# Thirty-two or sixty-four bytes more behind the weight tiles and the normed input's halves

## The chip, the cores and the metric

The kernel runs on one core of a Trainium2 chip. The metric is the device time of one execution in microseconds. Of the other cores none has work.

## The reference, cut to what matters

One layer of a hybrid decoder block on 256 tokens of width 2048, all in float32. Four large blocks of products follow each other, each behind an RMS norm:

```python
h = h + 0.5 * swiglu(rms_norm(h, ffn1_norm), ffn1_w_gu, ffn1_w_down)   # 2048 -> 2 x 5632 -> 2048
h = h + hybrid_mixer(rms_norm(h, mix_norm), w_in, ..., w_out)          # 2048 -> 7184 -> 2048
h = h + 0.5 * swiglu(rms_norm(h, ffn2_norm), ffn2_w_gu, ffn2_w_down)
gate = jax.nn.sigmoid(rms_norm(h, ple_norm) @ ple_w_gate)              # 2048 -> 2048
h = h + gate * (p @ ple_w_proj)                                        # 256 -> 2048
return rms_norm(h, final_norm)
```

The mixer holds a gated delta rule on eight heads and a stick-breaking attention on eight more; its own small products lie between the large ones.

## The kernel before, in words

Every large product is y = x @ w with 256 tokens in x. The tokens are the output's rows, in two tiles of 128; the columns of w go in blocks of 512, and the inner dimension in k-tiles of 128. TensorE has a stationary operand, which a weight load (LDWEIGHTS) brings in, and a moving one, which the matmul streams. Here **the stationary operand is x** (128 x 128, one k-tile of one tile of tokens) **and the moving operand is w** (128 x 512). So each matmul needs a weight load of its own, which runs beside the matmul ahead of it.

Both operands are split into two float32r halves, hi + lo, and three of the four products are taken: x_hi w_hi (line 73), x_hi w_lo (line 74) and x_lo w_hi (line 75). For the last block of columns of the last product lines 85 to 87 do the same for one tile of tokens after the other.

`weight_pair` (line 49) brings two k-tiles of a weight block, 512 KB, from DRAM into `raw` (four buffers, SyncE's queue), ScalarE rounds it to `whi` (line 59), and VectorE subtracts to get `wlo` (line 60). `whi` and `wlo` have three buffers each, so ScalarE and VectorE can be two pairs ahead of TensorE. `accumulate` (line 63) then issues 12 matmuls for the pair: two k-tiles, two tiles of tokens, three products.

The stationary halves have other names by stage. `nTh` and `nTl` are the normed and transposed input of a stage, four tiles each of four k-tiles, made by `new_nT` (line 109); they are used by the outputs `g` and `u` (gate and up columns of an FFN), `pj` (the mixer's input projection), `gt` (the last gate) and by the small `abT` (line 465, where `nTh` and `nTl` move and a padded tile `wpad` is stationary). `hTh` and `hTl` are the FFN's inner activations, used by `d`. `dnT` and `sbT` are the mixer's head outputs, used by `wo`. `ph` and `pl` are the embedding's input, used by `e`.

Between the pairs of a product a list of generators (`lanes`) puts in the pieces of other work: VectorE's transposes of the FFN's activations (line 127), the norms, and the mixer's heads. The order of instructions on each engine is the order in which the code emits them; tile pools give out the buffers, and a tile that is wanted again waits for the last reader of its buffer.

Tiles stand in each partition one behind the other in the order in which a pool first sees their tags, each at a multiple of 32 bytes. The sizes of nearly all large tiles are multiples of 512 bytes, so that all buffers of a tag, and all tags of a pool, have the same start modulo 512. In the built program the starts in bytes of a partition, modulo 512, are:

| tiles | operand of the large products | start modulo 512 |
|---|---|---|
| `raw`, `whi`, `wlo` | moving | 480 in all buffers |
| `nTh`, `nTl` | stationary of g, u, pj, gt | 480 in all tiles |
| `hTh`, `hTl` | stationary of d | 224 in all tiles |
| `dnT`, `sbT` | stationary of wo | 384 in all tiles |
| `ph`, `pl` | stationary of e | 224 |
| `wpad` | stationary of abT | 448 |
| `whi`, `wlo` of the last column block | moving, lines 85 to 87 | 224 in all buffers |

Inside a tile an operand starts at a multiple of 512 bytes from the tile's start, so a row of the table holds for every matmul of its stage.

Of the kernel before, what the change touches and what calls it, by code (L numbers as in the profile page):

```python
# [16 lines left out]
P = 128  # L17
T = 256
# [11 lines left out]
def block_kernel(ctx, tc, a, out):  # L30
# [17 lines left out]
    # ---------------------------------------------------------------- weights  # L48
    def weight_pair(src, pool=wp, bufs=3, parts=1):
        """Two k-tiles of a weight block, split into float32r halves hi + lo, in one or two parts."""  # L50
        raw = wp.tile([P, 2, NB], F32, tag="raw", name="raw", bufs=4)
        hi = pool.tile([P, 2, NB], F32R, tag="whi", name="whi", bufs=bufs)
        lo = pool.tile([P, 2, NB], F32R, tag="wlo", name="wlo", bufs=bufs)
        for i in range(parts):
            j = slice(2 * i // parts, 2 * (i + 1) // parts)
            nc.sync.dma_start(out=raw[:, j, :], in_=src[:, j, :])
        for i in range(parts):
            j = slice(2 * i // parts, 2 * (i + 1) // parts)
            nc.scalar.copy(hi[:, j, :], raw[:, j, :])  # L59
            nc.vector.tensor_tensor(out=lo[:, j, :], in0=raw[:, j, :], in1=hi[:, j, :], op=ALU.subtract)  # L60
        return hi, lo

    def accumulate(outs, xs, wsrc, nk, parts=1):
        """outs[t] += x[:, t].T @ w over nk k-tiles; xs(k) gives (hi, lo) [P, T]."""
        for g in range(nk // 2):
            whi, wlo = weight_pair(wsrc[g], parts=parts if g == 0 else 1)
            for j in range(2):
                k = 2 * g + j
                xh, xl = xs(k)
                for t in range(2):  # L70
                    c = slice(t * P, (t + 1) * P)
                    st, sp = k == 0, k == nk - 1
                    nc.tensor.matmul(outs[t], xh[:, c], whi[:, j, :], start=st, stop=False)  # L73
                    nc.tensor.matmul(outs[t], xh[:, c], wlo[:, j, :], start=False, stop=False)  # L74
                    nc.tensor.matmul(outs[t], xl[:, c], whi[:, j, :], start=False, stop=sp)  # L75
            lanes.step()

    def products(ps_t, t, xs, ws, n):
        """ps_t = x[:, t].T @ w[:, n] for one tile of tokens, with the pairs of weight tiles ws."""
        for g, (whi, wlo) in enumerate(ws):  # L80
            for j in range(2):
                k = 2 * g + j
                xh, xl = xs(k)
                c = slice(t * P, (t + 1) * P)
                nc.tensor.matmul(ps_t, xh[:, c], whi[:, j, n], start=k == 0, stop=False)
                nc.tensor.matmul(ps_t, xh[:, c], wlo[:, j, n], start=False, stop=False)
                nc.tensor.matmul(ps_t, xl[:, c], whi[:, j, n], start=False, stop=k == 2 * len(ws) - 1)

    # keeps the tensor engine's clock up until the first weights are there
# [6 lines left out]
    # ---------------------------------------------------------------- inputs  # L96
# [11 lines left out]
    # ---------------------------------------------------------------- norms  # L108
    def new_nT():
        hi = [act.tile([P, 4, T], F32R, tag="nTh", name="nTh", bufs=4) for _ in range(4)]  # L110
        lo = [act.tile([P, 4, T], F32R, tag="nTl", name="nTl", bufs=4) for _ in range(4)]
        return hi, lo
# [9 lines left out]
    def transpose_blocks(dst, src, q):  # L122
        """Tokens 32*q.. of both tiles: src [tokens, tile, 512] -> dst [column, k-tile, token], by 32 x 32."""
        for c in range(4):
            sv = src[32 * q:32 * q + 32].rearrange("p t (j c x) -> p t j c x", j=4, c=4)[:, :, :, c, :]
            dv = dst[32 * c:32 * c + 32].rearrange("p j (t q x) -> p t j q x", t=2, q=4)[:, :, :, q, :]
            nc.vector.transpose(dv, sv)  # L127

    def norm_block_behind(nT, which, j, tmp):
        """norm_block on the vector engine, emitted behind the next products."""  # L130
# [11 lines left out]
    def norm_block(nT, which, j, tmp):  # L142
        """Transposes columns j*512.. of h, times the norm's gain, into nT."""
# [29 lines left out]
    def rstd(stat, t=None):  # L173
        """1/sqrt(mean of h^2 + eps) by token, [P, 2] for both tiles or [P, 1] for tile t."""
# [8 lines left out]
    # ---------------------------------------------------------------- FFN  # L183
# [52 lines left out]
    # first norm: the transposed input comes from DRAM, its parts one after the other  # L236
# [43 lines left out]
    # ---------------------------------------------------------------- mixer  # L280
# [6 lines left out]
    # the embeddings' input, split ahead of its use  # L287
# [10 lines left out]
    # ---------------------------------------------------------------- per-layer embedding, last norm  # L298
    with tc.tile_pool(name="fin", bufs=1) as fp:
# [6 lines left out]
        def gated(e, gt, c, t, col):  # L306
            """Adds sigmoid(gt) * e to the columns c of h; their sum of squares into column col of stat."""
# [19 lines left out]
        # last columns: one tile of tokens after the other  # L327
# [18 lines left out]
class Lanes:  # L346
    """Work that is emitted piece by piece between the pairs of weight tiles of the large products."""
# [23 lines left out]
def mixer(tc, nc, a, act, mm_ps, mx_ps, accumulate, picker, new_nT, norm_block, sumsq, block, lanes,  # L371
# [5 lines left out]
    with tc.tile_pool(name="mix", bufs=1) as mp, \  # L377
            tc.tile_pool(name="dram", bufs=1, space=bass.MemoryType.DRAM) as dp:
        # ------------------------------------------------------------ constants
        one = mp.tile([P, 1], F32, tag="one", name="one")  # L380
        nc.gpsimd.memset(one, 1.0)
        # tri[j, i] = 1 where j <= i in the same half of 64
# [13 lines left out]
        # inverses of the triangular systems and (in part) their transposes, by tile and head: what is  # L396
        # below (above) the diagonal stays 0
# [5 lines left out]
        def natural(blk):  # L403
            """Columns blk*512.. of the input projection, [tokens, columns], two tiles."""
            o = [mm_ps("pj") for _ in range(2)]
            accumulate(o, xs, a["w_in"][blk], KD)
            return o
# [9 lines left out]
        def transpose_pair(nat, pr):  # L417
            """[tokens, 4 heads] -> PSUM [d, heads 2*pr and 2*pr+1, tokens]."""
# [13 lines left out]
        def bc(x):  # L432
            """[P, 4] -> [P, 4, 128], the same along the last axis."""
            return x.rearrange("p (c o) -> p c o", o=1).broadcast_to([P, 4, P])
# [13 lines left out]
        # ------------------------------------------------------------ decay and beta  # L448
# [5 lines left out]
        def decay_and_beta():  # L454
            wab = mp.tile([P, KD, 16], F32, tag="sol", name="wabr")
            nc.scalar.dma_start(out=wab, in_=a["w_ab"])
            # stationary columns: hi parts in 0..15, lo parts in 32..47
# [31 lines left out]
            # softplus(x) = max(x, 0) + ln(1 + exp(-|x|))  # L489
# [11 lines left out]
            # running sums of g inside halves of 64, and the sums of both halves  # L501
# [9 lines left out]
            # sB: running sum as seen from the second half; eG: exp of the sum from the tile's start;  # L511
            # eT: exp of the sum from here to the tile's end
# [9 lines left out]
        # ------------------------------------------------------------ gated delta rule: q, k, v of 4 heads  # L522
# [69 lines left out]
        # ------------------------------------------------------------ gated delta rule: the chain  # L592
# [4 lines left out]
        def chain(hg):  # L597
            hs = slice(hg * 4, hg * 4 + 4)
            kq, v, o = knq[hg], vn_[hg], o_nat[hg]
            # dec[j, t, head, i] = exp(sum of g over (j, i]), 0 where i < j  # L600
# [13 lines left out]
            # keys of the first tile, decayed to its end  # L614
            nc.vector.tensor_tensor(out=v3(kdec[hg]), in0=v3(kdec[hg]), in1=bc(eT[:, 0, hs]), op=ALU.mult)
            # AT[j, i] = (k_j . q_i) dec;  N[j, i] = -beta_j (k_j . k_i) dec
# [16 lines left out]
            # the diagonal blocks of 32, one per 4 partitions: [block (t c b), column group], rows x columns  # L633
# [12 lines left out]
            # forward substitution, 8 columns of an inverse in a partition  # L646
# [22 lines left out]
            # blocks of 32 -> blocks of 64  # L669
# [17 lines left out]
            # blocks of 64 -> 128  # L687
# [17 lines left out]
            # first tile: u = beta * (Z^T v); o = A u; state = k_dec^T u  # L705
# [13 lines left out]
            # second tile  # L719
# [18 lines left out]
            # o = rq d^-0.5 o, then the head norm: o times coef  # L738
# [18 lines left out]
        # ------------------------------------------------------------ stick-breaking  # L757
# [25 lines left out]
        def stick_a(hd):  # L783
# [6 lines left out]
            # sg = sigmoid(z), om = sigmoid(-z) = 1 - sigmoid(z), pr[s] = product of om over keys >= s;  # L790
            # columns: [tile 0 x keys of tile 0 | tile 1 x keys of tiles 0, 1]
# [4 lines left out]
            # on the diagonal tiles keep key < query  # L796
# [7 lines left out]
            # the last key of a tile is never attended to: its weight is 0 already  # L804
# [40 lines left out]
        # ------------------------------------------------------------ output gate  # L845
# [19 lines left out]
        # ------------------------------------------------------------ order of the products  # L865
# [16 lines left out]
        # ------------------------------------------------------------ output projection  # L882
# [4 lines left out]
        def pick(k):  # L887
            # order of the rows: delta rule 0-3, stick-breaking, delta rule 4-7
# [20 lines left out]
def _blocks(w, cols=NB):  # L909
    """[K, N] -> [N / 512, K / 256, 128, 2, 512]: pairs of k-tiles of a column block, each contiguous."""  # L910
# [49 lines left out]
```

## Time and profile before

| | us |
|---|---|
| time, median of 2 runs (2053.87 to 2054.19) | 2054.03 |
| span of the profiled execution, first to last instruction | 2052.8 |
| TensorE busy with matmuls | 2028.4 |
| TensorE weight loads, beside the matmuls | 1655.7 |
| VectorE busy | 1317.4 |
| ScalarE busy | 955.6 |
| GpSimd busy | 27.8 |

The profiled execution's own time is not given beside its span; the two timed runs lie 1.1 to 1.4 us above that span. A row of a group gives the line, the engine, the operation, the output and inputs by the program's names, the shape and the count, then busy time and mean nanoseconds of one, then idle time ahead of it. Of matmuls the duration is modelled and overlaps the next one's: how fast TensorE goes is read from the distance between the starts of two that follow each other. The order of time shows these starts to 0.01 us; over 12 matmuls that is good to about a nanosecond for each.

### The profile page before, as it was taken

The page shows a single profiled execution, that of the slowest core. Times are in us where ns is not written, and L with a number is a line of the kernel's source. Part 1 is how long each engine was busy: PE and PEld are TensorE (multiplying, and loading weights), DVE is VectorE, ACT ScalarE, POOL GpSimd, SP SyncE. Part 2 cuts the span into 40 slices and gives each one's busy share as a digit, 9 for nine tenths or more (in the row PEclk, how much of TensorE's full clock was granted, in tenths as well). Part 3 has the DMA queues.
Part 4 walks back from the last instruction along what each step waited for, and adds up shares of the span by engine and source line. Part 5 has one row for each costly group of instructions (what it writes and reads, how often), then busy time and mean ns, then how long its engine had stood idle before and what let it go on. Part 6 is the DMA issues. An engine that isn't in the chain of part 4 may idle for free. (4 is left out here: it accounts for less than half of the span.)

```text
span 2052.8 us, 24604 instructions
## 1 busy us (share of the span) xinstructions
PE 2028.4 (99%) x9256; PEld 1655.7 (81%) x9256; DVE 1317.4 (64%) x1786; ACT 955.6 (47%) x1194; POOL 27.8 (1%) x44
## 2 busy tenths in 40 slices
PE   9999999999999999999999999999999999999998
PEld 7778888877888888878878888888778888888887
DVE  5666666666556656794775776666666666666555
ACT  6444444444444457654545454444444443444454
POOL 0000000000000000000100000000000000000000
PEclk9999999999999999999999999999999999999999
DMA  8556656555665655554454565565566555665664
GB/s 294 178 185 195 194 187 193 185 175 187 202 196 193 195 183 165 177 183 143 147 179 139 176 196 187 191 189 190 175 190 195 189 191 189 195 192 184 210 191 156
DMA packets 112184, 382.80 MB, mean 186 GB/s; under 512 B 16833, under 2 KB 17857, under 8 KB 111937
## 3 DMA queue, kind: packets, MB, share of 16 engines
q1 hardware_dynamic: 110912, 379.76, 57.6%
q8 instruction: 72, 1.18, 0.2%
q10 hardware_dynamic: 1152, 1.47, 0.2%
q14 instruction: 48, 0.39, 0.1%
HBM read 378.56 MB, written 2.62 MB: 186 GB/s over the span
## 5 line engine op out<-in xcount | busy, mean ns | idle before, releaser
L60 DVE TENSOR_TENSOR wlo<-raw,whi 128x1024 fp32r<-128x1024 f32 (+1 forms) x709 | 863.1, 1222 | 644.8 <-ACT whi L59 641.0
L59 ACT CAST whi<-raw 128x1024 fp32r<-128x1024 f32 (+1 forms) x709 | 744.5, 1051 | 972.3 <-PE u L75 275.3
L74 PE MATMUL g<-wlo,nTh 128*128 128x512 f32 x704 | 281.6, 400 | 6.6 <-DVE wlo L60 4.7
L73 PE MATMUL g<-whi,nTh 128*128 128x512 f32 x704 | 274.4, 390 | 1.9 <-ACT whi L59 1.9
L74 PE MATMUL d<-wlo,hTh 128*128 128x512 f32 x704 | 274.6, 390 | 0.6 <-DVE wlo L60 0.4
L75 PE MATMUL g<-whi,nTl 128*128 128x512 f32 x704 | 274.8, 390 | 0.0
L73 PE MATMUL d<-whi,hTh 128*128 128x512 f32 x704 | 273.9, 389 | 0.0
L75 PE MATMUL d<-whi,hTl 128*128 128x512 f32 x704 | 273.9, 389 | 0.0
L73 PE MATMUL u<-whi,nTh 128*128 128x512 f32 x704 | 273.9, 389 | 0.0
L74 PE MATMUL u<-wlo,nTh 128*128 128x512 f32 x704 | 273.9, 389 | 0.0
L75 PE MATMUL u<-whi,nTl 128*128 128x512 f32 x704 | 273.9, 389 | 0.0
L73 PE MATMUL pj<-whi,nTh 128*128 128x512 f32 x448 | 180.0, 402 | 0.0
L74 PEld LDWEIGHTS g<-wlo,nTh 128*128 128x128 f32 x704 | 132.0, 188 | 59.2 <-DVE wlo L60 33.3
L74 PE MATMUL pj<-wlo,nTh 128*128 128x512 f32 x448 | 175.8, 393 | 3.1 <-DVE wlo L60 3.0
L75 PE MATMUL pj<-whi,nTl 128*128 128x512 f32 x448 | 175.5, 392 | 0.0
L127 DVE STREAM_TRANSPOSE tT<-sil 32x256 f32<-32x256 f32 x352 | 153.5, 436 | 6.1
L73 PEld LDWEIGHTS g<-whi,nTh 128*128 128x128 f32 x704 | 132.0, 188 | 30.8 <-ACT whi L59 2.5
L74 PEld LDWEIGHTS d<-wlo,hTh 128*128 128x128 f32 x704 | 132.1, 188 | 30.2 <-DVE wlo L60 3.2
L73 PEld LDWEIGHTS d<-whi,hTh 128*128 128x128 f32 x704 | 132.1, 188 | 27.6
L74 PEld LDWEIGHTS u<-wlo,nTh 128*128 128x128 f32 x704 | 132.1, 188 | 27.5
L75 PEld LDWEIGHTS d<-whi,hTl 128*128 128x128 f32 x704 | 132.1, 188 | 27.5
L73 PEld LDWEIGHTS u<-whi,nTh 128*128 128x128 f32 x704 | 132.1, 188 | 27.4
(250 smaller groups left out, 1771.1 us busy)
## 6 DMA issues: line engine op xcount, KB each, us to landing
raw<-in_w_gu SPq DMA_DIRECT2D x351, 512.0 KB, 4.2
raw<-in_w_down SPq DMA_DIRECT2D x176, 512.0 KB, 3.9
raw<-in_w_in SPq DMA_DIRECT2D x112, 512.0 KB, 3.5
raw<-in_w_out SPq DMA_DIRECT2D x32, 512.0 KB, 3.4
raw<-in_w_pg SPq DMA_DIRECT2D x32, 512.0 KB, 4.3
h<-in_x SPq DMA_DIRECT2D x8, 256.0 KB, 5.7
raw<-in_w_pp SPq DMA_DIRECT2D x4, 512.0 KB, 3.9
out_dram<-hf SPq DMA_DIRECT2D x8, 256.0 KB, 2.8
```

Of the source, the lines that this page charges most:

```text
L59: nc.scalar.copy(hi[:, j, :], raw[:, j, :])
L60: nc.vector.tensor_tensor(out=lo[:, j, :], in0=raw[:, j, :], in1=hi[:, j, :], op=ALU.subtract)
L73: nc.tensor.matmul(outs[t], xh[:, c], whi[:, j, :], start=st, stop=False)
L74: nc.tensor.matmul(outs[t], xh[:, c], wlo[:, j, :], start=False, stop=False)
L75: nc.tensor.matmul(outs[t], xl[:, c], whi[:, j, :], start=False, stop=sp)
L127: nc.vector.transpose(dv, sv)
```

## The change

The tiles `whi` and `nTh` get 8 float32 (32 bytes) more in each partition than their data, `wlo` and `nTl` get 16 (64 bytes) more, and the code works on the part without them.

```diff
     def weight_pair(src, pool=wp, bufs=3, parts=1):
         raw = wp.tile([P, 2, NB], F32, tag="raw", name="raw", bufs=4)
-        hi = pool.tile([P, 2, NB], F32R, tag="whi", name="whi", bufs=bufs)
-        lo = pool.tile([P, 2, NB], F32R, tag="wlo", name="wlo", bufs=bufs)
+        hi, lo = (pool.tile([P, 2 * NB + more], F32R, tag=tag, name=tag, bufs=bufs)[:, 0:2 * NB]
+                  .rearrange("p (j x) -> p j x", j=2) for tag, more in (("whi", 8), ("wlo", 16)))
...
     def new_nT():
-        hi = [act.tile([P, 4, T], F32R, tag="nTh", name="nTh", bufs=4) for _ in range(4)]
-        lo = [act.tile([P, 4, T], F32R, tag="nTl", name="nTl", bufs=4) for _ in range(4)]
-        return hi, lo
+        return tuple([act.tile([P, 4 * T + more], F32R, tag=tag, name=tag, bufs=4)[:, 0:4 * T]
+                      .rearrange("p (k x) -> p k x", k=4) for _ in range(4)] for tag, more in (("nTh", 8), ("nTl", 16)))
```

Comments and descriptions of functions are left out in the changed file, which moves no instruction. Each engine has the same instructions in the same order with the same waits and the same buffer numbers as before; behind `new_nT` their line numbers are smaller by one. What differs is where tiles stand:

| tiles | start modulo 512, before | after |
|---|---|---|
| `raw` | 480 | 480 |
| `whi` | 480 480 480 | 480 0 32 |
| `wlo` | 480 480 480 | 64 128 192 |
| `nTh` | 480 in all four | 256 288 320 352 |
| `nTl` | 480 in all four | 384 448 0 64 |
| `hTh`, `hTl` | 224 | 384 |
| `dnT`, `sbT` | 384 | 32 |
| `ph`, `pl` | 224 | 384 |
| `wpad` | 448 | 96 |
| `whi` of the last column block | 224 in all eight | 384 416 448 480 0 32 64 96 |
| `wlo` of the last column block | 224 in all eight | 128 192 256 320 384 448 0 64 |

The tiles that the diff doesn't name move because they stand behind those that grow.

Of the 8543 places where a large matmul streams while the weight load of the next one reads, the moving operand's start and that of the loaded one stand apart like this:

| distance of the two starts is a multiple of | before | after |
|---|---|---|
| 64 bytes | 8159 | 5382 |
| 128 bytes | 8159 | 2829 |
| 256 bytes | 8159 | 1493 |
| 512 bytes | 5856 | 256 |

Before, all those that are not at a multiple of 256 are the 383 in wo and one at its edge, at a distance of 96.

## The prediction

> **What bounds the kernel.** I read the page's first two parts, then the groups, then the waits, then the order of time of TensorE alone.
>
> ```profile
> span 2052.8 us, 24604 instructions
> ...
> PE 2028.4 (99%) x9256; PEld 1655.7 (81%) x9256; DVE 1317.4 (64%) x1786; ACT 955.6 (47%) x1194; POOL 27.8 (1%) x44
> ...
> PEclk9999999999999999999999999999999999999999
> ...
> L60 DVE TENSOR_TENSOR wlo<-raw,whi 128x1024 fp32r<-128x1024 f32 (+1 forms) x709 | 863.1, 1222 | 644.8 <-ACT whi L59 641.0
> L59 ACT CAST whi<-raw 128x1024 fp32r<-128x1024 f32 (+1 forms) x709 | 744.5, 1051 | 972.3 <-PE u L75 275.3
> ```
>
> TensorE is busy for 99% at full granted clock. VectorE and ScalarE, which make the weight halves, sit idle ahead of that work for 644.8 and 972.3 us. So the time is the number of large matmuls times the distance between two starts. That distance has to be read from the order of time:
>
> ```profile
> 399.66 0.39 PE L73 MATMUL u<-whi,nTh 128*128 128x512 f32 x1
> ...
> 402.38 0.39 PE L73 MATMUL u<-whi,nTh 128*128 128x512 f32 x1
> ```
>
> From the first to the last of these two rows 12 matmuls start (three products for each of two k-tiles and two tiles of tokens) in 2.72 us, **226.7 ns each**. The same count in the stage d takes as long, and in the stage wo longer:
>
> ```profile
> 599.88 0.39 PE L73 MATMUL d<-whi,hTh 128*128 128x512 f32 x1
> ...
> 602.60 0.39 PE L73 MATMUL d<-whi,hTh 128*128 128x512 f32 x1
> ```
>
> ```profile
> 1130.06 0.39 PE L73 MATMUL wo<-whi,sbT 128*128 128x512 f32 x1
> 1130.30 0.39 PE L74 MATMUL wo<-wlo,sbT 128*128 128x512 f32 x1
> 1130.53 0.40 PE L75 MATMUL wo<-whi,sbT 128*128 128x512 f32 x1
> 1130.76 0.39 PE L73 MATMUL wo<-whi,sbT 128*128 128x512 f32 x1
> ...
> 1132.86 0.39 PE L73 MATMUL wo<-whi,sbT 128*128 128x512 f32 x1
> ```
>
> d: 2.72 us for 12. wo: 2.80 us for 12, **233.3 ns each**, with the same shapes, the same moving tiles, the same engines at work beside it and no wait between the rows. By the table of starts, what sets wo apart is that its stationary tiles stand 96 bytes off the moving ones modulo 256; in u the distance is 0 and in d 256. The groups say the same for whole stages:
>
> ```profile
> L73 PE MATMUL u<-whi,nTh x704: 389/389/389, 30.1 to 1701.8; 128*128 128x512 f32 x176
> ```
>
> ```profile
> L73 PE MATMUL wo<-whi,dnT x64: 392/392/394, 1120.1 to 1209.9; 128*128 128x512 f32 x64
> L74 PE MATMUL wo<-wlo,dnT x64: 394/394/399, 1120.3 to 1210.1; 128*128 128x512 f32 x64
> L75 PE MATMUL wo<-whi,dnT x64: 392/399/399, 1120.6 to 1210.3; 128*128 128x512 f32 x64
> ```
>
> Minimum, median and maximum: 389 in all three for u, 392 to 399 in wo. So the start of a tile does matter to TensorE here, and the one stage with another residue is the slow one.
>
> **The change part by part.** No instruction, wait or buffer is added, so there is no new wait and nothing is queued otherwise. The only term is the distance between starts, at places where the change moves the two operands apart.
>
> The *price of one place* is wo's 233.3 less u's 226.7, 6.7 ns. Two more stretches bound it. The first is abT, whose stationary tile stands 32 bytes off the moving one; it has 256 columns, for which the products of the last block, 256 apart, are the measure:
>
> ```profile
> 2039.04 0.28 PE L85 MATMUL gt<-whi,nTh 128*128 128x256 f32 x1
> ...
> 2041.92 0.28 PE L85 MATMUL gt<-whi,nTh 128*128 128x256 f32 x1
> ```
>
> ```profile
> 755.66 0.39 PE L74 MATMUL pj<-wlo,nTh 128*128 128x512 f32 x1
> 755.89 0.40 PE L75 MATMUL pj<-whi,nTl 128*128 128x512 f32 x1
> 756.13 0.28 PE L465 MATMUL abT<-nTh,wpad 128*128 128x256 f32 x1
> 756.25 0.28 PE L466 MATMUL abT<-nTl,wpad 128*128 128x256 f32 x1
> 756.36 0.28 PE L465 MATMUL abT<-nTh,wpad 128*128 128x256 f32 x1
> 756.48 0.28 PE L466 MATMUL abT<-nTl,wpad 128*128 128x256 f32 x1
> 756.59 0.40 PE L73 MATMUL pj<-whi,nTh 128*128 128x512 f32 x1
> 756.83 0.40 PE L74 MATMUL pj<-wlo,nTh 128*128 128x512 f32 x1
> ```
>
> The last block needs 2.88 us for 24, 120.0 ns each. The matmul that streams while the first wpad is loaded (755.89) takes 0.24 where 0.227 is usual; the four of abT take 0.46 together, 115 ns each, some 5 less than 120; the next one needs 0.24 again. So a change of residue costs about 13 ns in one place and wins 5 in others.
>
> The second is what follows a wait. There the distance is 0, but TensorE has lost its step:
>
> ```profile
> 415.90 0.50 PE L74 MATMUL g<-wlo,nTh 128*128 128x512 f32 x1 [0.21 <-DVE wlo L60]
> 416.23 0.40 PE L75 MATMUL g<-whi,nTl 128*128 128x512 f32 x1
> ...
> 418.32 0.39 PE L75 MATMUL g<-whi,nTl 128*128 128x512 f32 x1
> ```
>
> From 416.23 to 418.32 nine matmuls start, 2.09 us, 232 ns each, before 226.7 comes back. I read this so: 226.7 is a step into which two streams fall when they meet at the same place each time, and out of step they cost 232 to 233. After the change `whi` and `wlo` alternate between residues with each matmul, so that hardly a row of three finds the same meeting twice. The price I take is therefore wo's 6.7 ns; the bounds are minus 13.3 ns (below) and plus 10, the longer of wo's steps.
>
> The lower bound comes from the two widths: 226.7 ns for 512 columns and 120.0 for 256 leave 106.7 for 256 columns, and 13.3 ns that do not depend on the width. More than these 13.3 can't be won.
>
> The *number of places*: by the table of the change 384 of 8543 are off a multiple of 256 before, 7050 after. So 6666 new ones, times 6.7 ns, is **44 us**.
>
> The *other engines* I cost at nothing. VectorE's subtraction takes 1222 ns with all three operands at 480; ScalarE has 1051. Should either grow by a tenth, 120 ns, it would still be hidden by the idle time quoted above, except where TensorE waits for the halves already:
>
> ```profile
> PEld g L74 <- DVE wlo L60: 33.3, 63, 1.0
> ```
>
> These waits come at the start of g's blocks, where VectorE is behind with the FFN's activations. A slower TensorE gives some of them back: a pair of weight tiles would take 0.08 us longer, and some three pairs pass in each of 22 blocks ahead of such waits, 5 us at most; I take 3. That is the only cover, and it cuts the loss. No transfer starts elsewhere: `raw` doesn't move.
>
> **Sum**: 2052.8 + 44 - 3 = 2094 against the profiled span; the median stands 1.2 us above the span, which gives **2095 us**, 2.0% slower.
>
> [...]
>
> **The rivals.**
>
> *Only the distance modulo 64 counts.* wo's 96 and abT's 32 are both 32 modulo 64, so the trace can't tell 64 from 256. Then 8543 - 5382 = 3161 places are off after the change, 2777 more than before, times 6.7 is 18.5 us: 2072. Against it speaks that the two don't cost the same.
>
> *Nothing happens*: wo's extra time has another cause than the start (its tiles come from other pools), or the step is found again at once. Then 2054. For it speaks that d is as fast as u, although 256 apart. This is also the case in which the change doesn't do what it says.
>
> *Faster.* The 13.3 ns are a collision of the load with the stream, and it is worst where both start at the same residue, as nearly everywhere now. Its place is each weight load beside a matmul, its price what the stagger spares: abT's 5 ns at 7050 places are 35 us, 2019; half of the 13.3 at all 8543 would be 57 us, 1997; all of it 114 us, 1940. It decides from the point at which the mean distance falls below 226.7. For it speak abT's four rows; against it wo, which is staggered and slower, and the rows on both sides of abT, which give back what it wins.
>
> [...]
>
> *Dearer*: with moving tiles that alternate, every place pays the 10 ns of the longer steps: 7050 x 10 = 71 us, 2125.
>
> **How the numbers follow.** The forecast has 0.46, its own range 2075 to 2112, since the price lies between 232 and 234 ns and some places fall into step; a bit more than half of that lies over 2095, where 2% ends. Modulo 64 has 0.12, nothing 0.12, faster 0.22 (0.18 of it below 2013), dearer 0.08. So faster by over 2% 0.18, within 2% 0.44 (0.17 of the forecast, both middle cases and the small gains), slower 0.38. Two per cent, 41 us, is about what a measurement of this kernel can tell from no change. The range goes from 1997, half the fixed part won, to 2130, just past the dearer case; some 0.15 is left out, most of it below.
>
> **What would show it.** In the changed profile the steps in u and d should lie near 232 to 233 ns, 2.78 to 2.80 us for 12, and u's durations should spread from 389 up to 399 as wo's do. wo, with 89 of 384 places at a multiple of 256, should go on near 233. The halves' 1222 and 1051 ns should stay. If u falls below 2.72 us for 12, the faster rival holds; if it stays, the residue was not the cause. The forecast is wrong above all if 233 is special to a distance of 96.

## Result and the profile after

The changed kernel takes 2080.97 us (2 runs, 2080.92 to 2081.01) against 2054.03: ratio 1.0131, 95% interval 1.0115 to 1.0147, so 27 us slower. It lies inside the forecast's own range, 2075 to 2112, and 14 us below its 2095.

The page after, the rows that answer to those of before:

```profile
span 2078.9 us, 24604 instructions
...
PE 2061.2 (99%) x9256; PEld 1658.5 (80%) x9256; DVE 1317.7 (63%) x1786; ACT 953.0 (46%) x1194; POOL 27.7 (1%) x44
...
PEclk9999999999999999999999999999999999999999
...
L60 DVE TENSOR_TENSOR wlo<-raw,whi 128x1024 fp32r<-128x1024 f32 (+1 forms) x709 | 863.4, 1223 | 670.3 <-ACT whi L59 666.4
L59 ACT CAST whi<-raw 128x1024 fp32r<-128x1024 f32 (+1 forms) x709 | 741.6, 1047 | 1001.0 <-PE u L75 286.5
```

The span grew by 26.1 us. The clock and the number of instructions are the same; VectorE's 1223 ns (1222 before) and ScalarE's 1047 (1051) do not move with the residues, and both engines sit idle a little longer. All of it is in TensorE's step. In the order of time a block of u and a stretch of d:

```profile
392.42 0.40 PE L73 MATMUL u<-whi,nTh 128*128 128x512 f32 x1
...
414.49 0.40 PE L75 MATMUL u<-whi,nTl 128*128 128x512 f32 x1
```

```profile
578.45 0.39 PE L73 MATMUL d<-whi,hTh 128*128 128x512 f32 x1
...
624.70 0.40 PE L75 MATMUL d<-whi,hTl 128*128 128x512 f32 x1
```

u: 95 matmuls start in 22.07 us, 232.3 ns each; d: 200 in 46.25 us, 231.3 ns. Before, both had 226.7. u's durations (minimum, median, maximum) no longer stand at one value:

```profile
L73 PE MATMUL u<-whi,nTh x704: 386/395/403, 29.7 to 1721.6; 128*128 128x512 f32 x176
```

How much of this reaches the end is seen by stage, from the first start of each stage's rows. Before (the start of wo, 1120.1, stands in the prediction), then after:

```profile
L73 PE MATMUL g<-whi,nTh x704: 387/389/499, 5.4 to 1680.1; 128*128 128x512 f32 x176
```

```profile
L73 PE MATMUL d<-whi,hTh x704: 388/389/397, 499.4 to 1942.4; 128*128 128x512 f32 x176
```

```profile
L73 PE MATMUL pj<-whi,nTh x448: 387/389/582, 740.0 to 1119.4; 128*128 128x512 f32 x150
```

```profile
L73 PE MATMUL g<-whi,nTh x704: 386/395/503, 5.4 to 1699.4; 128*128 128x512 f32 x176
```

```profile
L73 PE MATMUL d<-whi,hTh x704: 389/393/401, 505.3 to 1966.9; 128*128 128x512 f32 x176
```

```profile
L73 PE MATMUL pj<-whi,nTh x448: 387/396/586, 750.6 to 1132.9; 128*128 128x512 f32 x150
```

d of the first FFN took 240.6 us and takes 245.3, 4.7 more for 1056 matmuls, 4.5 ns each. Its g and u together took 494.0 and take 499.9: only 5.9 more for 2112 matmuls. At 4.7 ns each that would have been 9.9. By the order of time 2.7 us came back in g's waits, which got shorter; the other 1.3 are missing because g's steps between the waits had 227.9 ns on average before, not 226.7. What the waits show (engine and line, who is waited for, us, times, longest), one row before, then two after:

```profile
PE g L74 <- DVE wlo L60: 4.7, 21, 0.5
```

```profile
PEld g L74 <- DVE wlo L60: 29.3, 63, 1.0
...
PE g L74 <- DVE wlo L60: 0.5, 1, 0.5
```

Weight loads of g waited 33.3 us before, as the prediction shows. Take every 512-column matmul and the distance from its start to the next matmul's, and call it a wait where it is over 260 ns. Then the order of time gives 41.3 us of waits (beyond 226.7 ns each) before and 35.0 after, 6.4 less: 4.8 in g, 1.2 in pj, the rest elsewhere. The steps without a wait grew by 32.6 us. Together that is 26.2, next to the 26.1 of the span.

### The profile page after: what moved, and what is told of

It is laid out like the page before. It is cut to its first block, busy times and chain, and to the rows that moved or that the text cites. A ratio compares the mean times of both kernels' runs of the same rounds, so it can differ in the third digit from the quotient of the medians.

```text
span 2078.9 us, 24604 instructions
## 1 busy us (share of the span) xinstructions
PE 2061.2 (99%) x9256; PEld 1658.5 (80%) x9256; DVE 1317.7 (63%) x1786; ACT 953.0 (46%) x1194; POOL 27.7 (1%) x44
## 5 line engine op out<-in xcount | busy, mean ns | idle before, releaser
L60 DVE TENSOR_TENSOR wlo<-raw,whi 128x1024 fp32r<-128x1024 f32 (+1 forms) x709 | 863.4, 1223 | 670.3 <-ACT whi L59 666.4
L59 ACT CAST whi<-raw 128x1024 fp32r<-128x1024 f32 (+1 forms) x709 | 741.6, 1047 | 1001.0 <-PE u L75 286.5
L75 PEld LDWEIGHTS u<-whi,nTl 128*128 128x128 f32 x704 | 132.3, 188 | 31.1
```

## Experiments

All kernels are the one before with other sizes of tiles, so that instructions, order and waits stay. A step is read as the last start less the first, over the number of matmuls between.

### Each half of the change alone

`weights` pads whi and wlo alone, `inputs` nTh and nTl alone; one other tile (h for `weights`, stat for `inputs`) is made larger so that all else keeps its start modulo 512; its line is left out below.

```diff
# weights
-        hi = pool.tile([P, 2, NB], F32R, tag="whi", name="whi", bufs=bufs)
-        lo = pool.tile([P, 2, NB], F32R, tag="wlo", name="wlo", bufs=bufs)
+        hi = pool.tile([P, 2 * NB + 8], F32R, tag="whi", name="whi", bufs=bufs)[:, 0:2 * NB].rearrange("p (j x) -> p j x", j=2)
+        lo = pool.tile([P, 2 * NB + 16], F32R, tag="wlo", name="wlo", bufs=bufs)[:, 0:2 * NB].rearrange("p (j x) -> p j x", j=2)
# inputs: new_nT's two lines in the same way, with 8 and 16
```

> Only the weight halves get the extra bytes (whi 480 0 32, wlo 64 128 192 modulo 512); the room behind h is made 224 bytes larger so that nTh, nTl stand at 480, hTh, hTl at 224 and dnT, sbT at 384 as before. Theory (the step depends on how far the streamed operand and the operand loaded beside it stand apart, and 226.7 ns needs the same meeting each time): u, d, g and pj all go to 231 to 233 ns, 2075 to 2085 us. Rival (the normed input's own residues were what cost): 2054 us and u at 2.72 us for 12. Rival (modulo 64 is all that counts): only the whi buffer at 0 and the wlo buffers, which are off by 32 from the stationary 480 and 224, cost, so about 2/3 of the places, 2070 us.

> Only the normed input's halves get the extra bytes (nTh 480 0 32 64, nTl 96 160 224 288); all weight buffers stay at 480, hTh, hTl at 224, dnT, sbT at 384. Theory: g, u, pj and gt go to 231 to 233 ns, d stays at 2.72 us for 12 and wo at 2.80; less some us that the waits in g give back, 2066 to 2074 us. Rival (what costs is that the moving operand alternates between residues): all stays, 2054 us.

`weights`: 2084.45 us, ratio 1.0149 (1.0132 to 1.0166). `inputs`: 2075.08 us, ratio 1.0103 (1.0088 to 1.0118). In the order of time, u of `weights`, then u and d of `inputs`:

```profile
393.12 0.39 PE L73 MATMUL u<-whi,nTh 128*128 128x512 f32 x1
...
415.20 0.40 PE L75 MATMUL u<-whi,nTl 128*128 128x512 f32 x1
```

```profile
393.77 0.40 PE L73 MATMUL u<-whi,nTh 128*128 128x512 f32 x1
...
415.82 0.39 PE L75 MATMUL u<-whi,nTl 128*128 128x512 f32 x1
```

```profile
578.75 0.39 PE L73 MATMUL d<-whi,hTh 128*128 128x512 f32 x1
...
624.09 0.39 PE L75 MATMUL d<-whi,hTl 128*128 128x512 f32 x1
```

95 steps in 22.08 and 22.05 us: 232 ns in both. d, whose operands `inputs` leaves alone, has 200 in 45.34 us, 226.7. So it is not one side's residue alone that costs, and moving operands that all start alike don't save the step. The costs don't add: 31 and 21 us alone, 27 together. `weights` came out as forecast, `inputs` 1 us above its range.

### The same distances elsewhere, and one product of three moved

`shift` makes one constant 32 bytes larger, which moves all tiles behind it. `lo64` puts 64 bytes between whi and wlo, and makes h larger so that the stationary tiles keep their starts (that line is left out).

```diff
# shift
-    warm = cp.tile([P, 1], F32, tag="warm", name="warm")
+    warm = cp.tile([P, 16], F32, tag="warm", name="warm")[:, 0:1]
# lo64
+    gap = []
...
+        if pool is wp and not gap:
+            gap.append(wp.tile([P, 16], F32, tag="gap", name="gap"))
         lo = pool.tile([P, 2, NB], F32R, tag="wlo", name="wlo", bufs=bufs)
```

> Everything behind the constants stands 32 bytes later: raw, whi, wlo, nTh and nTl at 0 modulo 512, hTh, hTl at 256, dnT, sbT at 416; all distances are those of before. Theory (distance counts, not the place): 2054 us within 3, u and d at 2.72 us for 12 and wo at 2.80. Rival (a tile's own start counts, whether it is at a multiple of 64): u, d or wo change by several ns, 10 us or more in the time.

> Only wlo moves, by 64 bytes, to 32 modulo 512 in all its buffers; whi, nTh, nTl at 480, hTh, hTl at 224, dnT, sbT at 384. So one matmul of three streams from 64 bytes off, the same in each pair. Theory: the steps of u and d grow to 229 to 233 ns, 2065 to 2085 us. Rival (modulo 64): 2054 us, since 64 is a multiple. Rival (a fixed pattern is found again at once, whatever it is): 2054 us too; it parts from modulo 64 by the run weights.

`shift`: 2053.68 us, ratio 0.9999 (0.9990 to 1.0008), and u's 95 steps take 21.53 us, 226.7 ns, though every tile behind the constants stands 32 bytes later:

```profile
387.24 0.39 PE L73 MATMUL u<-whi,nTh 128*128 128x512 f32 x1
...
408.77 0.39 PE L75 MATMUL u<-whi,nTl 128*128 128x512 f32 x1
```

`lo64`: 2083.99 us, ratio 1.0146 (1.0131 to 1.0161); u takes 22.02 us for 95, 231.8 ns (the added lines move the line numbers by three):

```profile
393.18 0.39 PE L76 MATMUL u<-whi,nTh 128*128 128x512 f32 x1
...
415.20 0.39 PE L78 MATMUL u<-whi,nTl 128*128 128x512 f32 x1
```

With the distances kept, it made no difference to this step or to the time where the tiles stand. And one stream of three that stands off, by the same 64 bytes each time, lengthens all three steps: in u of the first FFN lines 76, 77 and 78 have 231.2, 232.2 and 232.5 ns on average, though only line 77 streams from 64 bytes off.

### One distance per stage

Three kernels give each stage one fixed distance (start of the streamed tile less start of the loaded one, modulo 256). Nothing is staggered; the room ahead of the stationary tiles differs.

```diff
# dist_a, where the lines that hand `more` to the FFN are left out: 128 in g, u, pj, gt; 32 and 64 in the two d; 0 in wo (dist_b, dist_c: other numbers in the same places)
-    h = act.tile([P, 2, D], F32, tag="h", name="h")
+    h = act.tile([P, 2 * D + 32], F32, tag="h", name="h")[:, 0:2 * D].rearrange("p (t x) -> p t x", t=2)
-                sil = fp.tile([P, 2, NB], F32, tag="sil", name="sil")
+                sil = fp.tile([P, 2 * NB + more], F32, tag="sil", name="sil")[:, 0:2 * NB].rearrange("p (t x) -> p t x", t=2)   # more: 24, then 16
-        one = mp.tile([P, 1], F32, tag="one", name="one")
+        one = mp.tile([P, 64], F32, tag="one", name="one")[:, 0:1]
```

> No stagger: every tag has one start in all its buffers, weights at 480. By larger tiles ahead of them the stationary tiles stand, moving less stationary modulo 256, at 128 in g, u, pj and gt, at 32 in d of the first FFN, at 64 in d of the second, and at 0 in wo. Theory (only 0 modulo 256 gives the short step): 231 to 234 ns in u and in both d, 226.7 ns in wo, which was 233.3 before; about 2085 us. Rival (modulo 128): u stays at 226.7. Rival (modulo 64): u and the second d stay at 226.7, only the first d is long, 2059 us. Rival (what costs is unequal starts of the buffers, not the distance): all of these stay at 226.7, 2054 us.

> The same with other distances: 160 in g, u, pj and gt, 192 in the first d, 224 in the second, 128 in wo. Theory: 231 to 234 ns in all of them, about 2090 us. Rival (modulo 128): wo at 226.7. Rival (modulo 64): the first d and wo at 226.7, the others long. Rival (unequal starts): 226.7 everywhere.

> The same with the distances left: 224 in g, u, pj and gt, 96 in the first d (that of wo before), 128 in the second, 32 in wo. Theory: 231 to 234 ns in all, and 233.3 in the first d, as wo had at 96. Rival (wo's long step is special to its tiles or stage): the first d at 226.7 and wo at 233. Rival (modulo 128): the second d at 226.7.

2082.67, 2096.34 and 2092.65 us, ratios 1.0139 (1.0120 to 1.0157), 1.0205 (1.0187 to 1.0224), 1.0187 (1.0169 to 1.0206). Of `dist_a` the second d at 64 and wo at 0, of `dist_c` the first d at 96 (wo's distance before), and of `dist_b` u at 160:

```profile
1799.21 0.39 PE L73 MATMUL d<-whi,hTh 128*128 128x512 f32 x1
...
1844.99 0.39 PE L75 MATMUL d<-whi,hTl 128*128 128x512 f32 x1
```

```profile
1167.57 0.39 PE L73 MATMUL wo<-whi,sbT 128*128 128x512 f32 x1
...
1183.89 0.39 PE L73 MATMUL wo<-whi,dnT 128*128 128x512 f32 x1
```

```profile
582.38 0.40 PE L73 MATMUL d<-whi,hTh 128*128 128x512 f32 x1
...
629.05 0.39 PE L75 MATMUL d<-whi,hTl 128*128 128x512 f32 x1
```

```profile
396.16 0.40 PE L73 MATMUL u<-whi,nTh 128*128 128x512 f32 x1
...
418.42 0.40 PE L75 MATMUL u<-whi,nTl 128*128 128x512 f32 x1
```

200 in 45.78 us, 72 in 16.32, 200 in 46.67, 95 in 22.26. Over all steps of a stage without a wait the means are as follows (a, b and c stand for `dist_a`, `dist_b` and `dist_c`):

| distance modulo 256 | 0 | 32 | 64 | 96 | 128 | 160 | 192 | 224 |
|---|---|---|---|---|---|---|---|---|
| ns from start to start | 226.7 (u before), 226.8 (wo, a) | 233.3 (d, a), 233.3 (wo, c) | 228.9 (d, a) | 233.3 (d, c; wo before) | 232.4, 232.9 (u, a), 233.3 (d, c), 232.4 (wo, b) | 234.3, 234.2 (u, b) | 233.3 (d, b) | 233.3 (d, b), 233.3 (u, c) |

Every distance off 0 that was tried costs, 64 least. The 64 at 2.2 ns missed its forecast of 231 to 234, though not as modulo 64 would have it; 128 falls with the rest, so modulo 128 is out too. u at 160 lies just above its forecast, and `dist_b` 6 us above its 2090. wo at 0 and d at 96 have changed places, so it was never wo's stage or pool.

### A stagger of 256 bytes, and distances of 4 and 16

```diff
# stag256
-        hi = pool.tile([P, 2, NB], F32R, tag="whi", name="whi", bufs=bufs)
+        hi = pool.tile([P, 2 * NB + 64], F32R, tag="whi", name="whi", bufs=bufs)[:, 0:2 * NB].rearrange("p (j x) -> p j x", j=2)
# fine: off is 1 in the first FFN, 4 in the second; tl alike
-                th = fp.tile([P, 4, T], F32R, tag="hTh", name="hTh", bufs=KF // 4)
+                th = fp.tile([P, 4 * T + 64], F32R, tag="hTh", name="hTh", bufs=KF // 4)[:, off:4 * T + off].rearrange("p (k x) -> p k x", k=4)
```

> A stagger of 256 bytes in place of 32: whi gets 64 float32 more per buffer, so that its buffers stand at 480, 224 and 480 modulo 512, wlo at 224, nTh and nTl at 224, hTh and hTl at 480; buffers of a tile lie at different residues modulo 512, but every distance between a stream and the operand loaded beside it stays a multiple of 256 (96 off it in wo, as before). Theory (modulo 256): nothing changes, u and d at 2.72 us for 12, 2054 us within 2. Rival (any change of residue from one matmul to the next loses the step): u and d at 231 to 233 ns, 2080 us.

> The FFN's inner halves hTh, hTl begin 4 bytes into their tiles in the first FFN and 16 bytes in the second (the tiles are 256 bytes larger, which keeps their starts); all else as before. Theory in its plain form (any distance off 256 costs): both d at 231 to 234 ns, about 2066 us. Rival (SBUF is read in lines of 32 or 64 bytes, and what lies inside a line does not matter): both d at 226.7, 2054 us. If 4 bytes keep 226.7 and 16 do not, the line is of 16 bytes or less.

`stag256`: 2054.34 us, ratio 1.0001 (0.9991 to 1.0010); u and d have 226.7 ns. Here buffers at different residues modulo 512 cost nothing, since all distances that were multiples of 256 stay so. `fine`: 2066.7 us, ratio 1.0060 (1.0041 to 1.0080); the d of the first FFN, 4 bytes off:

```profile
572.77 0.39 PE L73 MATMUL d<-whi,hTh 128*128 128x512 f32 x1
...
619.25 0.40 PE L75 MATMUL d<-whi,hTl 128*128 128x512 f32 x1
```

200 in 46.48 us, 232.4 ns; at 16 bytes 233.3. A distance of one element is enough to lose the 226.7 ns.

### The one stage that stood off, mended

```diff
-        one = mp.tile([P, 1], F32, tag="one", name="one")
+        one = mp.tile([P, 32], F32, tag="one", name="one")[:, 0:1]
```

> The kernel before with one small tile of the mixer made 96 bytes larger, so that dnT and sbT stand at 480 like the weights. Theory: wo falls from 2.80 us for 12 to 2.72, 383 steps times 6.7 ns, 2.6 us less: 2051.4 us. Rival (wo is long for another reason): 2054 us and 2.80.

```profile
1148.71 0.39 PE L73 MATMUL wo<-whi,sbT 128*128 128x512 f32 x1
...
1165.03 0.39 PE L73 MATMUL wo<-whi,dnT 128*128 128x512 f32 x1
```

72 in 16.32 us, 226.7 ns where the kernel before had 233.3; 2051.96 us, ratio 0.9989 (0.9980 to 0.9998). The gain is small, 2.2 us, but it makes this the fastest of the kernels: the extra bytes bring the two operands' starts together, where the change moved them apart.

The same kernel tells which load is the partner of a stream: the one that runs beside it, or the matmul's own, one step earlier. `wpad` moves too, to 32 modulo 512. So of the pj matmul ahead of abT nothing but the distance to the load beside it changes, from 32 to 192 modulo 256; its own nTl stays at distance 0. The prediction shows it before, from 755.89 to 756.13. Here:

```profile
755.24 0.39 PE L75 MATMUL pj<-whi,nTl 128*128 128x512 f32 x1
755.47 0.28 PE L465 MATMUL abT<-nTh,wpad 128*128 128x256 f32 x1
```

In all six such places without a wait this matmul takes 226 ns, where the kernel before, `shift`, `stag256` and `fine` have 235 in all six. So the load beside the stream counts. A single place at 192 costs nothing here, while 192 throughout a stage costs 6.6 ns.

## Why the prediction was right, and where it was off

- **The cause** was named rightly and is shown: in these runs the step of a float32r matmul of 512 columns depends on the distance modulo 256 between its stream and the operand that is loaded beside it (held throughout a stage: 226.7 to 226.8 ns at 0, 228.9 to 234.3 ns at the others of the table). `shift` keeps the distances and the time (ratio 0.9999); `dist_a` to `dist_c` change the distances alone; `stag256` changes residues modulo 512 but keeps the distances modulo 256 and costs nothing (ratio 1.0001). In u, d and wo the stationary tiles come to TensorE by weight loads alone (704 of 188 ns each for line 73 of u), so a load has to be the partner. That it is the load beside the stream was read in the prediction from the pj matmul next to abT, and `mended` bears it out: 226 ns where the kernel before has 235, with only that load's distance changed. A run without the load was not made.
- **The picture behind it** does not hold as it was put: that 226.7 is the step when two streams "meet at the same place each time". In `dist_a` to `dist_c` they meet at the same place each time too, and take 228.9 to 234.3 ns wherever that place is not 0 modulo 256. Meeting alike is not enough; of the distances held throughout a stage only multiples of 256 gave the short step (226.7 ns in u before, 226.8 in d before and in wo of `dist_a`).
- **The price** was the step that was mis-sized: wo's 6.7 ns was taken for all. It holds where a distance off 0 is *fixed* at 32, 96, 192 or 224, but the change makes the distances vary from pair to pair, and there u and d have 231.3 to 231.5 ns on average over the whole stage, 4.7 more. The prediction's own row for a lost step, 232 ns after a wait, was nearer than wo's. Nor is there one price for a place by itself: 64 bytes throughout a stage cost 2.2 ns (`dist_a`), 64 bytes at one place of three cost 5.3 ns on every step of u (`lo64`), and 192 bytes at one place alone cost nothing (`mended`).
- **The number of places** was too low, and it was luck that this made up for part of the price's error: the 1493 places that stay at a multiple of 256 don't keep 226.7 ns. In u and d of the first FFN 312 such steps (by the addresses of the built program) have 230.6 ns on average; `lo64` shows too that neighbours count. At 4.7 ns the 7840 steps without a wait outside wo come to 37 us. g and pj had 227.9 and 228.3 ns before, between their waits, and so had less to lose, and wo got 1.2 ns shorter: 32.6 us by the order of time, not 44.
- **The waits** gave back 6.4 us, not 3: 4.8 in g, near the 5 that the prediction gave as the most, and 1.2 in pj, which it did not count.
- **The rivals**: modulo 64 (2072) falls with `dist_a`, where 64 is the cheapest but not free and 128 costs 5.7 to 6.7 ns, and with `lo64`, 2083.99 us where it gives 2054. Nothing happens: falls with 1.0131. Faster: no distance tried had a shorter step than 226.7; abT's four short rows were not a promise for 512 columns. Dearer: the longest mean of a stage in any run is 234.4 (e in `dist_b`), 7.7 above 226.7 and not 10. The chances as told add up to 0.45 for within 2% and 0.37 for slower, where 0.44 and 0.38 are given.
- wo went on near 233 as said: 232.2 on average.

Why multiples of 256 bytes are the good distances, and why 64 is cheaper than 32 (228.9 against 233.3 ns), stays open; no run here looks below the start times.

## What to carry to other kernels

Where each float32r matmul of 512 columns reloads its stationary operand, as here, read the distance between starts stage by stage; in this kernel two stages of one shape with different steps, u's 226.7 and wo's 233.3 ns, pointed to where their tiles stood. Try the streamed and the loaded tiles at the same start modulo 256 in every stage, which a pad of a few floats in a pool's first tile did in `mended`: wo's step went from 233.3 to 226.7 ns. Before staggering tiles to avoid a conflict, measure the kernel with equal starts too. A slower TensorE is partly paid by waits that it had anyway: 6.4 of 32.6 us here.

## What was not expected

One element, 4 bytes, of distance costs nearly as much as 32 bytes do (232.4 against 233.3 ns). And the narrow matmuls of the last block went the other way: where 256 columns took 120.0 ns at a distance of 256, the changed kernel, with most distances off it, takes less:

```profile
2064.84 0.28 PE L85 MATMUL gt<-whi,nTh 128*128 128x256 f32 x1
...
2067.68 0.28 PE L85 MATMUL gt<-whi,nTh 128*128 128x256 f32 x1
```

24 in 2.84 us, 118.3 ns. Over the whole block the mean is 119.9 before and in every run that keeps its distances, 118.1 in the changed kernel, 117.5 in `weights` and 118.8 in `inputs`. abT's matmuls, also of 256 columns, went up instead, from 117.5 ns at their 32 bytes to 119.1. So what holds for 512 columns can't be carried to 256; no run gave the narrow ones one fixed distance after another.
